# A hybrid decoder step on one core: the last chunk of the down pass takes four pairs, its products are staggered, and the residual stream lies in two tiles

## Chip, cores and metric

The kernel runs on one core of a Trainium2 chip. The metric is device time of one execution in microseconds; lower is better.

## The reference

One layer of a decoder on 1,024 prompt tokens and 64 sample tokens (1,088 rows of width 1,024), in float32:

```python
x = layer_norm(ALPHA * x + 0.5 * swiglu(x, f1_wg, f1_wu, f1_wd), ln1_g, ln1_b)
z = x @ w_in + b_in                 # split into u, v, q, k, vm, o, ig, fg
...                                 # gMLP groups and mLSTM heads on z -> mix
x = layer_norm(ALPHA * x + mix @ w_out, ln2_g, ln2_b)
x = layer_norm(ALPHA * x + 0.5 * swiglu(x, f2_wg, f2_wu, f2_wd), ln3_g, ln3_b)
```

with `swiglu(x, wg, wu, wd) = (silu(x @ wg) * (x @ wu)) @ wd` and a hidden width of 2,816.

## The kernel before

The rows are nine tiles of 128 tokens: 0 to 7 are the prompt, 8 holds the 64 sample tokens. Each feed-forward layer has an up pass (class `Up`, lines 340 to 400) and a down pass (class `Down` and function `down`). The hidden width is 22 blocks of 128, taken as 11 pairs.

Both passes use seven products of half matrices instead of eight (a Strassen-like scheme), numbered 1 to 7 and taken in the order `DOWN_ORDER = (1, 2, 6, 5, 3, 7, 4)`. A product has a left operand made of hidden activations (`hop`, written to memory by the up pass as `hw` and loaded back, 512 KB each) and a right operand made of weights (`wop`). Each operand is split into a high and a low part, so one product over one pair is three matmuls of 128x512 (`PROD`, line 682). The `wop` is made by a cast on ScalarE (line 221) and a subtraction on VectorE (line 222).

The 11 pairs are cut into chunks. Within a chunk, a round is one product number for four row blocks `i`: block `i` stands for tiles `i` and `i + 4`. The pairs of the chunk add up in PSUM, and at the end of each product VectorE adds the PSUM tile to the residual stream `y` (line 653). Products 1, 6, 7 and 4 of a block share one PSUM tile (`px`, named `pd`); 2, 5 and 3 take one of a ring of four (`pw`), and the sample tokens' products another of that ring (`psm`, line 691). Product 5 is added twice, to tile `i + 4` and to tile `i`; product 3 goes to tile `i`.

In the last chunk each tile's last addition also collects its sum (`finish`) and starts a background task that normalises the tile (`layer_norm`, lines 266 to 290): a sum of squares on ScalarE, a power on GpSimd, two whole-row operations on VectorE. After the first pass the task then transposes the tile on TensorE (line 235) and splits it into `xt`; after the second it stores the tile, and tile 7 alone goes by statistics in two halves (line 674). The sample tile is folded first (`fold_tail`, line 766). The projection that follows the first pass (`zunit`, line 872, PSUM `po`) takes the tiles one after the other and waits for each one's task.

Operands are prepared ahead: three `wop` (`DOWN_AHEAD`) beyond the round, from nine buffers, and `hop` by SyncE's queue two further on into a ring of eight. `y` is loaded from the residual in quarter-megabyte pieces at the beginning of a pass, into memory that the up pass has left. The Python code makes the instructions in the order of its loops, and a scheduler in the tile framework then orders each engine's queue; so what stands where is read from the built program.

Of the kernel before, what the change touches and what calls it, by code (L numbers as in the profile page):

```python
# [43 lines left out]
UP_ORDER = (1, 2, 6, 5, 7, 3, 4)  # L44
DOWN_ORDER = (1, 2, 6, 5, 3, 7, 4)
NPRE = 2
CHUNKS = ((0, 1), (2, 3, 4), (5, 6, 7), (8, 9, 10))
PROD = ((0, 0), (0, 1), (1, 0))
UP_AHEAD = 3
DOWN_AHEAD = 3  # L50
# [51 lines left out]
class Weights:  # L102
# [32 lines left out]
    def done(self, n):  # L135
        for i in range(self.finished, self.finished + n):
            self.tiles.pop(self.plan[i])
        self.finished += n
        self.fill()


class Background:
# [25 lines left out]
def trunk_kernel(ctx: ExitStack, tc: tile.TileContext, a):  # L168
# [39 lines left out]
    def psum_s(name):  # L208
        return pss.tile([P, 512], F32, tag="s", name=name)
# [335 lines left out]
    class Down:  # L545


        def __init__(self, ffn):
            self.ffn = ffn
            self.items = [(ci, m, pair) for ci, pairs in enumerate(CHUNKS) for m in DOWN_ORDER for pair in pairs]  # L550
            self.n = 0
            self.raws, self.t1s, self.ops, self.hsl, self.hops = {}, {}, {}, {}, {}
            self.ud = None

        def load(self, group):
            if group in self.raws or 2 * group >= NPAIR:
# [27 lines left out]

        def fetch(self, upto):
            while self.fetched < min(upto, len(self.items)):
                _, m, pair = self.items[self.fetched]
                self.hop_load(unit(self.ud, "hop", f"hop{pair}_{m}"), pair, m)
                self.fetched += 1

        def prepare(self, upto):
# [47 lines left out]
    def down(dn, residual, on_tile):  # L639
# [18 lines left out]
        for ci, pairs in enumerate(CHUNKS):  # L658
# [34 lines left out]
                                  skip_group_check=True)  # L693

            px = {}
            smp = None

            rounds = [[(m, i) for i in range(4)] for m in DOWN_ORDER]
            if last:
                rounds[5:] = [[(m, i) for i in range(4) for m in DOWN_ORDER[5:]]]  # L700
            for r, round_ in enumerate(rounds):
                ms = sorted({m for m, i in round_}, key=DOWN_ORDER.index)
                done[0] += len(pairs) * len(ms)
# [6 lines left out]
                if ci == 0 and r == 3:  # L710
                    load_y(residual, range(4, 8), (0,))
                late = ci == 0 and r < 2
                for sm in (() if late and r == 0 else (1, 2) if late else ms):
                    if sm in (1, 2, 3, 7):
                        if sm in (1, 3):
                            smp = psum_s("psm")
                        sample(smp, sm, {1: 0, 2: 1, 3: 2, 7: 0}[sm], sm in (1, 3))
                        if sm in (2, 7):
                            add(smp, 8, int(sm == 7))
                if last and 7 in ms:  # L720
                    sums8 = lnst.tile([P, 1], F32, tag="sums8", name="sums8", bufs=1)
                    bg.spawn("fold", fold_tail(sums8))
# [3 lines left out]
                for m, i in round_:  # L726
                    if m in (1, 6, 7, 4):
                        if m == 1:
                            px[i] = psum_z("pd")
                        p = px[i]  # L730
                        product(p, m, i, m == 1)
                    else:
                        p = psum_s("pw")
                        product(p, m, i, True)
                    if m == 1:
                        add(p, i, 0)
                    elif m == 2:
                        finish(p, i, 0)
                    elif m == 6:
                        add(p, i, 1)  # L740
                    elif m == 5:
                        add(p, i + 4, 1)
                        add(p, i, 1)
                    elif m == 3:
                        finish(p, i, 1)
                        if last:
                            bg.spawn(("ln", ffn + 1, i), on_tile(i, sums[i]))
                    elif m == 7:
                        finish(p, i + 4, 1)
                    else:  # L750
                        finish(p, i + 4, 0)
                        if last:
                            bg.spawn(("ln", ffn + 1, i + 4), on_tile(i + 4, sums[i + 4]))
                    bg.tick()
                for m in ms:
                    for pair in pairs:
                        dn.hops.pop((pair, m))
# [10 lines left out]

    def y_pool(name):
        yp = tc.alloc_tile_pool(name=name, bufs=1, reuse_waits="tile")  # L770
        st["y"] = yp.tile([P, NT, YW], F32, tag="y", name="y")
        return yp


# [157 lines left out]

    wts = token_weights("o", 0)
    G.memset(y[TS:P, 8, :], 0.0)
    for t in range(NT):
        rows = _rows(t)
        bg.until(("ln", 1, t))

        def evict(p, t=t, rows=rows):
            add_psum(t, zg[:rows, t, :], p[:, 0:8], gb[:rows])  # L940
            og = m2.tile([P, 256], F32, tag="og", name="og")
            add_psum(t, og[:rows], p[:, 8:264], bc1[:rows, 0:256])
            S.activation(y[:rows, t, 520:776], og[:rows], AF.Tanh, scale=0.5)

        zunit(t, wts, 264, evict, "po", release=t == 8)

    def gtile(name, shape=(NT, H)):
        return mx.tile([P] + list(shape), F32, tag="g_" + name, name="g_" + name)
# [292 lines left out]
    def epilogue_a(h):  # L1241
# [4 lines left out]
        V.reciprocal(dn, dn)  # L1246
        yield
        hv = hh[:, :, 0:P]
        yo = y[:, :, 520 + h * P:520 + (h + 1) * P]
        dnb = dn.unsqueeze(2).to_broadcast([P, NT, P])  # L1250
        if h == 2:
            V.tensor_tensor(yo, hv, dnb, op=ALU.mult)
        else:
            V.tensor_tensor(hv, hv, dnb, op=ALU.mult)
            yield
            if h == 3:
                while ("o", 1) not in bg.finished:
                    yield
            V.scalar_tensor_tensor(yo, yo, 1.0, hv, op0=ALU.add, op1=ALU.mult)
        yield  # L1260
        bg.spawn(("epb", h), epilogue_b(h))

# [397 lines left out]
```

## Time and profile before

| | us |
|---|---|
| median of three runs | 2012.18 (2011.77 to 2012.43) |
| profiled execution | 2008.55 |
| its span | 2006.8 |
| TensorE busy | 1945.1 (97%) |
| VectorE busy | 1333.6 (66%) |

The span is that of one execution under the hardware profiler, with times from its start; the first down pass runs from 482 to 739 us, the second from 1747 to 1993. A row of the timeline gives start, duration, engine, line and operation, what is written and read, the count of merged instructions, and in brackets the idle time just before them and what ended it. Matmuls overlap, so one reads longer (about 0.4 us) than the distance between two.

### The profile page before, as it was taken

The page shows a single profiled execution, that of the slowest core. Times are in us where ns is not written, and L with a number is a line of the kernel's source. Part 1 is how long each engine was busy: PE and PEld are TensorE (multiplying, and loading weights), DVE is VectorE, ACT ScalarE, POOL GpSimd, SP SyncE. Part 2 cuts the span into 40 slices and gives each one's busy share as a digit, 9 for nine tenths or more (in the row PEclk, how much of TensorE's full clock was granted, in tenths as well). Part 3 has the DMA queues.
Part 4 walks back from the last instruction along what each step waited for, and adds up shares of the span by engine and source line. Part 5 has one row for each costly group of instructions (what it writes and reads, how often), then busy time and mean ns, then how long its engine had stood idle before and what let it go on. Part 6 is the DMA issues. An engine that isn't in the chain of part 4 may idle for free.

```text
span 2006.8 us, 27421 instructions
## 1 busy us (share of the span) xinstructions
PE 1945.1 (97%) x10263; PEld 1648.5 (82%) x10263; DVE 1333.6 (66%) x2337; ACT 766.1 (38%) x1499; POOL 489.4 (24%) x404
## 2 busy tenths in 40 slices
PE   8999999998999989999999999999999999989996
PEld 7888888887788869888978999888888888868885
DVE  8866565665866594366775767986655565676558
ACT  6544444443222241154454233644444444322122
POOL 0222322223421130104332510113222222153112
PEclk9999999999999999999999999999999999999999
DMA  5444433348865552111111073234444433897554
GB/s 211 150 170 149 148 130 120 129 146 312 342 243 188 184 177 65 43 43 51 43 50 55 26 236 117 90 130 151 142 153 161 133 127 109 292 378 253 178 176 147
DMA packets 105501, 308.64 MB, mean 154 GB/s; under 512 B 19736, under 2 KB 27416, under 8 KB 102552
## 3 DMA queue, kind: packets, MB, share of 16 engines
q1 hardware_dynamic: 83192, 226.13, 34.2%
q10 hardware_dynamic: 22176, 80.75, 10.1%
q8 instruction: 81, 1.33, 0.3%
q14 instruction: 52, 0.43, 0.1%
HBM read 205.50 MB, written 101.34 MB: 153 GB/s over the span
## 4 chain that ended last, share of the span: by engine, by line
PE 82%; DVE 8%; DMA 3%; ACT 2%; POOL 2%; issue 2%; ACTq 0%; DVEq 0%; SPq 0%; POOLq 0%
PE px L364 23%; PE pw L364 12%; PE pd L682 11%; PE pw L682 8%; PE pz L364 6%; PE pw L872 4%; PE psm L380 4%; PE pq L892 4%; DMA hd<-hw 3%; PE pv L872 2%; PE po L872 2%; PE psm L691 2%; PE pgm L872 1%; DVE y L290 1%; PE tp L235 1%
## 5 line engine op out<-in xcount | busy, mean ns | idle before, releaser
L364 PE MATMUL px<-xo,uop 128*128 128x512 f32 x2112 | 504.5, 394 | 6.1 <-ACT uop L355 6.1
L364 PEld LDWEIGHTS px<-xo,uop 128*128 128x128 f32 x2112 | 392.4, 188 | 91.6 <-ACT uop L355 6.3
L682 PE MATMUL pd<-wop,hop 128*128 128x512 f32 x1056 | 255.4, 398 | 6.8 <-ACT wop L221 3.4
L356 DVE TENSOR_TENSOR uop<-ur,uop 128x512 fp32r<-128x512 f32 x264 | 187.2, 730 | 101.2 <-ACT uop L355 101.0
L364 PE MATMUL pw<-xo,uop 128*128 128x512 f32 x1056 | 250.0, 392 | 0.0
L682 PEld LDWEIGHTS pd<-wop,hop 128*128 128x128 f32 x1056 | 199.7, 190 | 55.1 <-ACT wop L221 4.3
L364 PEld LDWEIGHTS pw<-xo,uop 128*128 128x128 f32 x1056 | 198.1, 188 | 44.3
L682 PE MATMUL pw<-wop,hop 128*128 128x512 f32 x792 | 191.2, 397 | 8.8 <-DVE y L653 7.5
L355 ACT CAST uop<-ur 128x512 fp32r<-128x512 f32 x264 | 157.0, 620 | 97.4 <-PE psm L380 65.3
L682 PEld LDWEIGHTS pw<-wop,hop 128*128 128x128 f32 x792 | 149.5, 189 | 45.2 <-DVE y L653 8.4
L221 ACT CAST wop<-wd 128x512 fp32r<-128x512 f32 x132 | 80.9, 620 | 261.4 <-DVE y L653 187.1
L345 POOL TENSOR_TENSOR s<-ur,ur 128x1024 f32<-128x1024 f32 x18 | 43.3, 2403 | 509.6 <-DVE uop L356 436.3
L222 DVE TENSOR_TENSOR hw<-c,hw 128x512 fp32r<-128x512 f32 x132 | 108.0, 818 | 80.0 <-ACT hw L221 79.9
L653 DVE SCALAR_TENSOR_TENSOR y<-y,pd 128x512 f32<-128x512 f32 x128 | 85.9, 682 | 65.2 <-PE pd L682 65.1
L364 PE MATMUL pz<-xo,uop 128*128 128x512 f32 x528 | 127.7, 397 | 0.0
L222 DVE TENSOR_TENSOR wop<-wd,wop 128x512 fp32r<-128x512 f32 x132 | 108.5, 829 | 23.9 <-ACT wop L221 23.1
L221 ACT CAST hw<-c 128x512 fp32r<-128x512 f32 x132 | 82.0, 621 | 109.6 <-DVE c L470 48.1
L653 DVE SCALAR_TENSOR_TENSOR y<-y,pw 128x512 f32<-128x512 f32 x128 | 84.0, 684 | 55.6 <-PE pw L682 55.6
L364 PEld LDWEIGHTS pz<-xo,uop 128*128 128x128 f32 x528 | 97.5, 188 | 22.4
L380 PEld LDWEIGHTS psm<-uop,xs 128*128 128x128 f32 x704 | 95.3, 189 | 7.8 <-ACT uop L355 0.3
L872 PE MATMUL pgm<-w,xt 128*128 128x256 f32 x768 | 99.8, 287 | 1.8 <-POOL w L123 0.8
L872 PE MATMUL pw<-w,xt 128*128 128x256 f32 x768 | 99.2, 287 | 0.3 <-ACT xt L221 0.3
(299 smaller groups left out, 2878.6 us busy)
## 6 DMA issues: line engine op xcount, KB each, us to landing
hd<-hw ACTq DMA_DIRECT2D x154, 512.0 KB, 3.4
hop<-hd SPq DMA_DIRECT2D x154, 512.0 KB, 5.0
ur<-in_wu SPq DMA_DIRECT2D x94, 512.0 KB, 3.8
wd<-in_wd SPq DMA_DIRECT2D x22, 1024.0 KB, 8.5
wr<-in_ws SPq DMA_DIRECT2D x76, 256.0 KB, 2.9
hsd<-sm SPq DMA_DIRECT2D x22, 192.0 KB, 4.1
y<-in_x SPq DMA_DIRECT2D x16, 256.0 KB, 6.2
x1d<-y SPq DMA_DIRECT2D x8, 512.0 KB, 4.0
```

The lines of the kernel that those rows point to most:

```text
L221: S.copy(hi, src)
L222: V.tensor_sub(dst[ix + (1,)], src, hi.bitcast(F32))
L345: eng.tensor_tensor(s1, a21, a22, op=ALU.add)
L355: S.copy(op[:, 0], sj)
L356: V.tensor_sub(op[:, 1], sj, op[:, 0].bitcast(F32))
L364: TE.matmul(ps, lhsT=units[k // 2][:, wi, c0:c0 + P], rhs=self.xo[m][:, k, xi, :], start=start and k == 0 and j == 0, stop=k == 3 and j == ...
L380: TE.matmul(ps, lhsT=self.xs[:, which, k, :], rhs=units[k // 2][:, wi, (k % 2) * 256:(k % 2 + 1) * 256], start=first and k == 0 and wi == ...
L653: V.scalar_tensor_tensor(yv, yv, al, p, op0=ALU.mult, op1=ALU.add, **(dict(accum_out=accum) if accum is not None else {}))
L682: TE.matmul(p, lhsT=hop[:, hi, i * P:(i + 1) * P], rhs=wop[:, wi, :], start=start and pi == 0 and j == 0, stop=pi == len(pairs) - 1 and j ...
L691: TE.matmul(p, lhsT=hsl[pair][:, which, :], rhs=wop[:, wi, :], start=start and pi == 0 and wi == 0, stop=pi == len(pairs) - 1 and wi == 1, ...
L872: TE.matmul(p[:, :n], lhsT=xl(t, k, xi), rhs=wk[:, wi, kk * n:(kk + 1) * n], start=(i == 0), stop=(i == last - 1))
L892: TE.matmul(p[:, :n], lhsT=wk[:, wi, kk * P:(kk + 1) * P], rhs=rhs, start=(i == 0), stop=(i == (23 if c < 2 else 15)), skip_group_check=c ...
```

## The change

The chunks are cut at other places: 2, 3, 2 and 4 pairs instead of 2, 3, 3 and 3. In all chunks but the last, products 5 and 3 are one double round, staggered (5 of block 0, 5 of 1, 3 of 0, 5 of 2, 3 of 1, ...): product 3 accumulates in PSUM on top of product 5 after 5 has been added to tile `i + 4`, and tile `i` gets both in one addition. The sample products of that round move behind it. In the last chunk 7 and 4 are staggered in the same way, where the code took them alternately, and the `hop` of product 7 lie in one larger tile (`hopx`). `y` becomes two tiles, one for tiles 0 to 3 and one for 4 to 8, behind a small class that picks by tile; operations over all nine tiles are issued once for each part. The first projection takes tile 8 fifth instead of last.

```diff
-CHUNKS = ((0, 1), (2, 3, 4), (5, 6, 7), (8, 9, 10))
+CHUNKS = ((0, 1), (2, 3, 4), (5, 6), (7, 8, 9, 10))
...
+class Tokens:
+    def __getitem__(self, ix):
+        rows, t, cols = ix
+        return self.first[rows, t, cols] if t < 4 else self.second[rows, t - 4, cols]
+    def parts(self, cols):
+        return (slice(0, 4), self.first[:, :, cols]), (slice(4, NT), self.second[:, :, cols])
...
-                _, m, pair = self.items[self.fetched]
-                self.hop_load(unit(self.ud, "hop", f"hop{pair}_{m}"), pair, m)
+                ci, m, pair = self.items[self.fetched]
+                if ci == len(CHUNKS) - 1 and m == 7:
+                    if self.hopx is None:
+                        self.hopx = xa_tile(xap, "hopx")
+                    hop = self.hopx[:, pair - CHUNKS[-1][0]]
+                else:
+                    hop = unit(self.ud, "hop", f"hop{pair}_{m}")
+                self.hop_load(hop, pair, m)
...
+            def staggered(m1, m2):
+                return [(m1, 0)] + [x for i in range(3) for x in ((m1, i + 1), (m2, i))] + [(m2, 3)]
...
             if last:
-                rounds[5:] = [[(m, i) for i in range(4) for m in DOWN_ORDER[5:]]]
+                rounds[5:] = [staggered(*DOWN_ORDER[5:])]
+            else:
+                rounds[3:5] = [staggered(*DOWN_ORDER[3:5])]
+            pw = {}
...
+                if ms != [5, 3]:
+                    samples(() if late and r == 0 else (1, 2) if late else ms)
...
+                    elif m == 3 and not last:
+                        p = pw.pop(i)
+                        product(p, m, i, False)
                     else:
-                        p = psum_s("pw")
+                        p = pw[i] = psum_s("pw")
                         product(p, m, i, True)
...
                     elif m == 5:
                         add(p, i + 4, 1)
-                        add(p, i, 1)
+                        if last:
+                            add(p, i, 1)
...
+                if ms == [5, 3]:
+                    samples(ms)
...
-        st["y"] = yp.tile([P, NT, YW], F32, tag="y", name="y")
+        st["y"] = Tokens(yp.tile([P, 4, YW], F32, tag="ya", name="ya"), yp.tile([P, NT - 4, YW], F32, tag="yb", name="yb"))
...
-    for t in range(NT):
+    for t in (0, 1, 2, 3, 8, 4, 5, 6, 7):
...
-        zunit(t, wts, 264, evict, "po", release=t == 8)
+        zunit(t, wts, 264, evict, "po", release=t == 7)
...
-        yo = y[:, :, 520 + h * P:520 + (h + 1) * P]
+        yos = y.parts(slice(520 + h * P, 520 + (h + 1) * P))
...
-            V.scalar_tensor_tensor(yo, yo, 1.0, hv, op0=ALU.add, op1=ALU.mult)
+            for ts, yo in yos:
+                V.scalar_tensor_tensor(yo, yo, 1.0, hv[:, ts], op0=ALU.add, op1=ALU.mult)
```

Where instructions now stand is shown at three places. Lines of the changed kernel are 15 to 40 higher than before, and numbers behind a name tell buffers apart.

TensorE at the end of the first down pass, before: the last product of 4 (`pd_5274`, tile 7), then transposes (`tp`) of tiles 4, 5 and 6, then the projection (`po`) of tile 0 from `xt00` and `xt01`.

```order
L682 MATMUL pd_5274<-wop8_4_5617,hop8_4_5488 128x512 x3
L682 MATMUL pd_5274<-wop9_4_5621,hop9_4_5494 128x512 x3
L682 MATMUL pd_5274<-wop10_4_5625,hop10_4_5614 128x512 x3
L235 MATMUL tp_5744<-cc_76,y_3948 128x128 x4
L235 MATMUL tp_5755<-cc_76,y_3948 128x128 x4
L235 MATMUL tp_5789<-cc_76,y_3948 128x128 x4
L235 MATMUL tp_5799<-cc_76,y_3948 128x128 x4
L872 MATMUL po_6003<-w0_5875,xt00_5554 128x264
L235 MATMUL tp_5833<-cc_76,y_3948 128x128 x4
L235 MATMUL tp_5843<-cc_76,y_3948 128x128 x4
L872 MATMUL po_5904<-w0_5875,xt00_5554 128x264 x5
L872 MATMUL po_5904<-w1_5880,xt00_5554 128x264 x6
```

The same place in the changed kernel: `po_5863`, `po_5910` and `po_5941` are tiles 0, 1 and 2, and the transposes that read `yb` are those of tiles 4 and 5.

```order
L703 MATMUL pd_5135<-wop10_4_5573,hop10_4_5562 128x512 x3
L910 MATMUL po_5863<-w0_5834,xt00_5478 128x264 x4
L250 MATMUL tp_5714<-cc_76,yb_3949 128x128 x4
L250 MATMUL tp_5725<-cc_76,yb_3949 128x128 x4
L910 MATMUL po_5863<-w0_5834,xt00_5478 128x264 x2
L250 MATMUL tp_5765<-cc_76,yb_3949 128x128 x4
L250 MATMUL tp_5775<-cc_76,yb_3949 128x128 x4
L910 MATMUL po_5863<-w1_5839,xt00_5478 128x264 x6
L910 MATMUL po_5863<-w2_5844,xt01_5492 128x264 x6
L910 MATMUL po_5863<-w3_5849,xt01_5492 128x264 x6
L910 MATMUL po_5910<-w0_5834,xt00_5478 128x264 x6
L910 MATMUL po_5910<-w1_5839,xt00_5478 128x264 x6
```

The transposes of tiles 4 and 5 now stand between projection matmuls, and those of tile 6 have moved behind 59 of them, where before one stood ahead.

TensorE near the end of the second down pass, before: `pd_16935` is the PSUM tile of block 0, `pd_16946` of block 1, `pd_16957` of block 2 and `pd_16968` of block 3; the number behind `wop` and its pair is the product.

```order
L682 MATMUL pd_16957<-wop8_7_17179,hop8_7_17118 128x512 x3
L682 MATMUL pd_16957<-wop9_7_17185,hop9_7_17123 128x512 x3
L682 MATMUL pd_16957<-wop10_7_17191,hop10_7_17176 128x512 x3
L682 MATMUL pd_16968<-wop8_7_17179,hop8_7_17118 128x512 x3
L682 MATMUL pd_16968<-wop9_7_17185,hop9_7_17123 128x512 x3
L682 MATMUL pd_16968<-wop10_7_17191,hop10_7_17176 128x512 x3
L682 MATMUL pd_16935<-wop8_4_17281,hop8_4_17182 128x512 x3
L682 MATMUL pd_16935<-wop9_4_17285,hop9_4_17188 128x512 x3
L682 MATMUL pd_16935<-wop10_4_17289,hop10_4_17278 128x512 x3
L682 MATMUL pd_16946<-wop8_4_17281,hop8_4_17182 128x512 x3
L682 MATMUL pd_16946<-wop9_4_17285,hop9_4_17188 128x512 x3
L682 MATMUL pd_16946<-wop10_4_17289,hop10_4_17278 128x512 x3
```

In the changed kernel the four blocks' tiles are `pd_16765`, `pd_16779`, `pd_16793` and `pd_16807`, and each product is over four pairs.

```order
L703 MATMUL pd_16807<-wop7_7_17080,hopx_17009 128x512 x3
L703 MATMUL pd_16807<-wop8_7_17085,hopx_17009 128x512 x3
L703 MATMUL pd_16765<-wop7_4_17202,hop7_4_17088 128x512 x3
L703 MATMUL pd_16765<-wop8_4_17208,hop8_4_17193 128x512 x3
L703 MATMUL pd_16765<-wop9_4_17212,hop9_4_17199 128x512 x3
L703 MATMUL pd_16765<-wop10_4_17216,hop10_4_17205 128x512 x3
L703 MATMUL pd_16779<-wop7_4_17202,hop7_4_17088 128x512 x3
L703 MATMUL pd_16779<-wop8_4_17208,hop8_4_17193 128x512 x3
L703 MATMUL pd_16779<-wop9_4_17212,hop9_4_17199 128x512 x3
L703 MATMUL pd_16779<-wop10_4_17216,hop10_4_17205 128x512 x3
L703 MATMUL pd_16807<-wop9_7_17091,hopx_17009 128x512 x3
L703 MATMUL pd_16807<-wop10_7_17196,hopx_17009 128x512 x3
```

Product 4 of blocks 0 and 1 has moved ahead of the second half of product 7 of block 3; after product 4 of block 0 there are now 42 matmuls to the end, 27 before.

VectorE at the very end of the second pass, before: line 290 is the last step of a tile's normalisation, 287 the step before, 653 the addition of a product, and 674 to 283 the statistics and halves of tile 7.

```order
L290 SCALAR_TENSOR_TENSOR y_15643<-y_15643,bmv_17370,bc_ln3_b_17214 128x1024
L674 BN_STATS bst_17416<-y_15643 128x6
L226 TENSOR_SCALAR rsq_17406<-bmv_17400 128x1
L287 SCALAR_TENSOR_TENSOR y_15643<-y_15643,bmv_17400,bc_ln3_g_17212 128x1024
L653 SCALAR_TENSOR_TENSOR y_15643<-y_15643,pd_16968 128x512
L290 SCALAR_TENSOR_TENSOR y_15643<-y_15643,bmv_17400,bc_ln3_b_17214 128x1024
L674 BN_STATS bst_17416<-y_15643 128x6
L259 BN_AGGR bmv_17432<-bst_17416 128x2
L261 TENSOR_SCALAR bmv_17432<-bmv_17432 128x1
L226 TENSOR_SCALAR rsq_17436<-bmv_17432 128x1
L280 SCALAR_TENSOR_TENSOR y_15643<-y_15643,bmv_17432,bc_ln3_g_17212 128x512 x2
L283 SCALAR_TENSOR_TENSOR y_15643<-y_15643,bmv_17432,bc_ln3_b_17214 128x512 x2
```

In the changed kernel the same steps are lines 305, 302, 674 and 695 to 298; the first row is tile 7's last addition.

```order
L674 SCALAR_TENSOR_TENSOR yb_15622<-yb_15622,pd_16807 128x512
L283 SCALAR_TENSOR_TENSOR bmv_17361<-sums_17308,negd_79 128x1
L695 BN_STATS bst_17344<-yb_15622 128x6
L274 BN_AGGR bmv_17384<-bst_17344 128x2
L276 TENSOR_SCALAR bmv_17384<-bmv_17384 128x1
L295 SCALAR_TENSOR_TENSOR yb_15622<-yb_15622,bmv_17384,bc_ln3_g_17117 128x512
L241 TENSOR_SCALAR rsq_17367<-bmv_17361 128x1
L302 SCALAR_TENSOR_TENSOR yb_15622<-yb_15622,bmv_17361,bc_ln3_g_17117 128x1024
L241 TENSOR_SCALAR rsq_17388<-bmv_17384 128x1
L295 SCALAR_TENSOR_TENSOR yb_15622<-yb_15622,bmv_17384,bc_ln3_g_17117 128x512
L305 SCALAR_TENSOR_TENSOR yb_15622<-yb_15622,bmv_17361,bc_ln3_b_17119 128x1024
L298 SCALAR_TENSOR_TENSOR yb_15622<-yb_15622,bmv_17384,bc_ln3_b_17119 128x512 x2
```

Behind tile 7's last addition there now stand tile 6's normalisation (`bmv_17361`) and tile 7's own steps; before, the end of tile 5's (`bmv_17370`, the first row) and the first step of tile 6's (`bmv_17400`) stood ahead of that addition.

More of the change, by code (lines that the diff above doesn't have):

```diff
@@ L139, in done, with __init__ @@
         self.fill()
+class Tokens:
+    def __init__(self, first, second):
+        self.first, self.second = first, second
+    def __getitem__(self, ix):
[3 more added lines that the diff above has]
+        return (slice(0, 4), self.first[:, :, cols]), (slice(4, NT), self.second[:, :, cols])
 class Background:
@@ L552, in __init__ @@
             self.raws, self.t1s, self.ops, self.hsl, self.hops = {}, {}, {}, {}, {}
-            self.ud = None
+            self.ud = self.hopx = None
         def load(self, group):
@@ L695, in down @@
             px = {}
-            smp = None
+            smp = []
+            def staggered(m1, m2):
+                return [(m1, 0)] + [x for i in range(3) for x in ((m1, i + 1), (m2, i))] + [(m2, 3)]
             rounds = [[(m, i) for i in range(4)] for m in DOWN_ORDER]
             if last:
-                rounds[5:] = [[(m, i) for i in range(4) for m in DOWN_ORDER[5:]]]
+                rounds[5:] = [staggered(*DOWN_ORDER[5:])]
+            else:
+                rounds[3:5] = [staggered(*DOWN_ORDER[3:5])]
+            pw = {}
             for r, round_ in enumerate(rounds):
@@ L712, in down, with samples @@
                 late = ci == 0 and r < 2
[L713 to L719, printed above, removed]
+                def samples(sms):
+                    for sm in sms:
+                        if sm in (1, 2, 3, 7):
+                            if sm in (1, 3):
+                                smp.append(psum_s("psm"))
+                            sample(smp[-1], sm, {1: 0, 2: 1, 3: 2, 7: 0}[sm], sm in (1, 3))
+                            if sm in (2, 7):
+                                add(smp[-1], 8, int(sm == 7))
+                if ms != [5, 3]:
+                    samples(() if late and r == 0 else (1, 2) if late else ms)
                 if last and 7 in ms:
@@ L1248, in epilogue_a @@
         hv = hh[:, :, 0:P]
-        yo = y[:, :, 520 + h * P:520 + (h + 1) * P]
+        yos = y.parts(slice(520 + h * P, 520 + (h + 1) * P))
         dnb = dn.unsqueeze(2).to_broadcast([P, NT, P])
         if h == 2:
-            V.tensor_tensor(yo, hv, dnb, op=ALU.mult)
+            for ts, yo in yos:
+                V.tensor_tensor(yo, hv[:, ts], dnb[:, ts], op=ALU.mult)
         else:
@@ L1258, in epilogue_a @@
                     yield
-            V.scalar_tensor_tensor(yo, yo, 1.0, hv, op0=ALU.add, op1=ALU.mult)
+            for ts, yo in yos:
+                V.scalar_tensor_tensor(yo, yo, 1.0, hv[:, ts], op0=ALU.add, op1=ALU.mult)
         yield
```

## The prediction

> **What bounds the kernel now.** I read the page's head first, then the stretches of both down passes as windows, then TensorE in order of time wherever a window shows it idle, and last VectorE at those places. The head says that TensorE is the bound.
>
> ```profile
> span 2006.8 us, 27421 instructions
> PE 1945.1 (97%) x10263; PEld 1648.5 (82%) x10263; DVE 1333.6 (66%) x2337; ACT 766.1 (38%) x1499; POOL 489.4 (24%) x404
> ```
>
> Nothing in the change removes a matrix product, so it can only pay out of the 61.7 us in which TensorE is idle, or where the clock is low. The windows give stretch, length, busy time of TensorE (PE), weight loads, VectorE, ScalarE, GpSimd, and then the granted clock.
>
> ```profile
> 546.00:704.00 158.00, 158.00 (x682) 127.88 (x681) 95.36 (x144) 33.56 (x54) 33.60 (x22) 1.00 0.60 208
> 1810.00:1972.00 162.00, 162.00 (x703) 131.56 (x702) 98.02 (x150) 34.16 (x55) 33.69 (x23) 1.00 0.58 199
> 735.30:750.40 15.10, 7.29 (x39) 5.55 (x37) 14.91 (x26) 8.75 (x15) 6.84 (x21) 0.91 0.64 213
> 747.80:754.60 6.80, 5.83 (x27) 5.86 (x28) 6.39 (x9) 2.10 (x4) 0.76 (x5) 0.50 0.96 321
> 1982.30:1984.30 2.00, 0.02 (x2) 0.05 (x1) 2.00 (x7) 0.60 (x1) 0.00 (x0) 1.00 0.00 0
> 1992.90:2006.80 13.90, 0.00 (x0) 0.00 (x0) 10.36 (x18) 1.24 (x2) 3.87 (x3) 0.65 0.38 151
> ```
>
> The inner chunks of both passes have no gap at all (158 of 158, 162 of 162). The losses are where the first pass hands over to the projection (735 to 750: VectorE busy 14.91 of 15.10, TensorE 7.29), the 2 us at 1982, and the 13.9 us after the last matmul. VectorE ends the waits in all three; behind the first the clock is at half for 6.8 us.
>
> **The change part by part.**
>
> *Third product accumulated on the fifth, staggered.* Twelve additions per pass go (four in each of three chunks), 24 in all at 0.684 us, 16.4 us of VectorE.
>
> ```profile
> L653 DVE SCALAR_TENSOR_TENSOR y<-y,pw 128x512 f32<-128x512 f32 x128 | 84.0, 684 | 55.6 <-PE pw L682 55.6
> ```
>
> All lie in the inner chunks where TensorE never waits, and VectorE itself waits 55.6 us before this group: gain 0. What it may cost: the third product of a row of tokens now needs the fifth's first addition to have read the buffer. One other product stands between, six to nine matmuls at 0.231 us (16.64/72, the row next below), 1.4 to 2.1 us, against 0.68. The double round also keeps six operands (hop) in the ring of eight in the one three-pair chunk of each pass.
>
> ```profile
> 1910.17 16.64 PE pd L682 x72
> L567 SPq DMA_DIRECT2D hop<-hd x51: 319/320/873, 546.2 to 694.2; - x51
> DMA to landing us min/median/max: 3.5/4.4/6.3
> ```
>
> The third hop of product 3 can be loaded when the last product of round 6 frees a unit: 2.1 us, then two fifth products (4.2) and two thirds of the next (1.4), 7.7 us ahead of its use. Landing takes 4.4, at most 6.3. I take 0, bounds 0 and 3 us of loss (two such rounds).
>
> *Last chunk of four pairs.* The number of matmuls is the same. Three operands are prepared ahead of a round, so the fourth pair's cast and subtraction fall into the round.
>
> ```profile
> L221 ACT CAST wop<-wd 128x512 fp32r<-128x512 f32 x132 | 80.9, 620 | 261.4 <-DVE y L653 187.1 <-PE pd L682 43.4 <-PE pw L682 16.5
> L222 DVE TENSOR_TENSOR wop<-wd,wop 128x512 fp32r<-128x512 f32 x132 | 108.5, 829 | 23.9 <-ACT wop L221 23.1
> ```
>
> That is 1.45 us; the first product reaches its fourth pair after 9 matmuls, 2.1 us, and with seven of nine operand buffers in use the two engines may begin before the round does. I take 0; bounds 0 and 0.6 us at each of ten round heads, 6 us.
>
> *Hand-over of the first pass.* Seven waits, of which these are the rows (the eighth is the slow run of projection matmuls behind them, the last the same at full clock).
>
> ```profile
> 722.45 1.09 PE L235 MATMUL tp<-cc,y 128*128 128x128 f32 x8 [0.67 <-DVE rsq L226]
> 727.32 1.06 PE L235 MATMUL tp<-cc,y 128*128 128x128 f32 x8 [1.47 <-DVE bmv L266]
> 736.38 0.36 PE L872 MATMUL po<-w,xt 128*128 128x264 f32 x1 [0.64 <-DVE y L653]
> 736.90 2.37 PE L682 MATMUL pd<-wop,hop 128*128 128x512 f32 x9 [0.16 <-DVE y L653]
> 740.70 2.26 PE L235 MATMUL tp<-cc,y 128*128 128x128 f32 x16 [1.43 <-DVE y L290]
> 744.84 0.36 PE L872 MATMUL po<-w,xt 128*128 128x264 f32 x1 [1.89 <-DVE rsq L226]
> 748.77 1.94 PE L235 MATMUL tp<-cc,y 128*128 128x128 f32 x8 [3.57 <-DVE y L290]
> 750.36 10.49 PE L872 MATMUL po<-w,xt 128*128 128x264 f32 x69
> 762.83 13.34 PE L872 MATMUL po<-w,xt 128*128 128x264 f32 x108
> 732.70 0.67 DVE L653 SCALAR_TENSOR_TENSOR y<-y,pd 128x512 f32<-128x512 f32 x1
> 735.54 0.69 DVE L653 SCALAR_TENSOR_TENSOR y<-y,pd 128x512 f32<-128x512 f32 x1 [0.19 <-PE pd L682]
> ```
>
> They sum to 9.83 us. Now the transposes of tiles 4 to 6 stand ahead of nearly all projection matmuls, so TensorE sits until VectorE has normalised those tiles. In the changed order they stand between projection matmuls of tiles 0 to 3 and 8. I place each against E, the end of the last down product.
>
> Tile 4: its addition at 732.70 to its transposes at 740.70 was 8.0 us. Its last product now ends 40 matmuls (9.2) and eight short transposes (0.7) before E, its transposes come 0.5 after: covered. Tile 5: its addition follows 0.6 later and its transposes 1.1 later, 8.5 us; its last product ends 28 matmuls, 6.5 us, before E, its transposes stand 1.6 after: wait 0.4. Tile 6: 735.54 to 748.77 was 13.2; now 2.8 before E (12 matmuls) and 59 projection matmuls (13.34/108 = 0.124 each, 7.3) and 16 transposes (2.1) after, 12.2: wait 1.0. So 1.4 us are left, a gain of 8.4. If tiles 4 and 5 also took 13.2, the three would wait up to 5 us together: bounds 4.8 and 9.8.
>
> The clock: 69 matmuls took 10.49 where 69 x 0.124 = 8.5, and eight transposes 1.94 where the row at 722 has 1.09. With no wait over 1.0 us I expect no low clock: gain 2.8, bounds 0 and 3.5. The Trainium skill (TensorE: Matmul & The Clock Gate, section on the HAM clock gate) says that the clock is halved after an idle window of about 3.4 us, windows running free of the program. By it the 6.8 us at half would give back 3.4 instead of 2.8; the trace agrees in that half clock begins at the 3.57 us wait.
>
> *Round of 7 and 4 in the second pass.*
>
> ```profile
> 1984.29 8.56 PE L682 MATMUL pd<-wop,hop 128*128 128x512 f32 x36 [1.98 <-issue]
> 1983.51 0.67 DVE L653 SCALAR_TENSOR_TENSOR y<-y,pd 128x512 f32<-128x512 f32 x1
> ```
>
> The first product of 4 waited for the addition of 7 at 1983.51, which stood behind normalisations of tiles 0 to 3. Now 50 matmuls instead of 42 stand between (1.85 us more), and round 3 gives VectorE 2.77 instead of 2.08 us a tile (2.8 us less backlog); against it three subtractions come in ahead (2.5). 1.98 - 1.85 - 2.8 + 2.5 is below 0; I leave 0.3: gain 1.7, bounds 0 and 2.
>
> *After the last matmul* (1984.29 + 8.56 = 1992.85) VectorE works until the last row here ends at 2003.64, 10.8 us, and the store takes 3.2.
>
> ```profile
> 1993.19 1.27 DVE L287 SCALAR_TENSOR_TENSOR y<-y,bmv,bc_ln_g 128x1024 f32<-128x1024 f32 x1
> 1996.11 0.69 DVE L674 BATCH_NORM_STATS2 bst<-y 128x6 f32<-128x512 f32 x1
> 1997.96 0.68 DVE L653 SCALAR_TENSOR_TENSOR y<-y,pd 128x512 f32<-128x512 f32 x1
> 2000.47 0.21 DVE L259 BATCH_NORM_AGGREGATE bmv<-bst 128x2 f32<-128x12 f32 x1
> 2002.23 1.41 DVE L283 SCALAR_TENSOR_TENSOR y<-y,bmv,bc_ln_b 128x512 f32<-128x512 f32 x2
> ```
>
> Tile 5's normalisation and all of tile 6's lie in it. In the new order the product of tile 4 ends 42 matmuls (9.7 us) before E instead of 27 (6.2), that of tile 5 30 instead of 18, so both are done by E. What is left: addition of tile 7 (0.6), its statistics (0.7) and aggregation (0.4), four half rows at about 0.7 (2.8), two whole rows of tile 6 (2.4), five tiny steps and their latencies (0.9): 7.8. Gain 3.0, bounds 1.5 and 3.5.
>
> *Two tiles for the residual stream.* The first pass also has waits at its start:
>
> ```profile
> 499.64 2.92 PE L682 MATMUL pw<-wop,hop 128*128 128x512 f32 x6 [5.40 <-DVE y L653]
> SPq L637 <- PE pw L364: 8.9, 1, 8.9
> ```
>
> The residual's loads wait for product 3 of the up pass, whose operand lies where y goes. The first half, 4 x 1040 x 4 = 16,640 bytes a partition, is 256 bytes longer than an operand tile and still touches the next, so its first load still waits: gain 0, and 5.4 us if it did not. The split VectorE operations of the heads (one more for each of four heads) run beside a busy TensorE: 0.
>
> Sum: 8.4 + 2.8 + 1.7 + 3.0 = 15.9 us. The profiled execution took 2008.55 us, of which the span is 2006.8; it becomes 1990.9 in span and 1992.65 in all. The median of the runs is 3.63 above that execution, so 2012.18 - 15.9 = 1996.3.
>
> **The rivals.** *The hand-over stays VectorE-bound* (chance 0.14): VectorE was busy 14.91 of 15.10 us there and no normalisation is removed. For it: the same work per tile. Against it: the five tiles' projection is 13.8 us of ready matmuls. With waits of 5 and the low clock kept: 4.8 + 0 + 1.7 + 3.0 = 9.5 us, 2002.7.
>
> *The fourth pair's operand comes late* (0.05), the case on the other side: ten round heads. It decides once cast and subtraction end more than 2.1 us after the head; each us beyond costs 10 us, so at 2.1 us beyond (the subtraction behind three queued additions) 21 us are lost and 2017 results. Against it: VectorE is busy 95.36 of 158.
>
> *The residual does load early* (0.04): another 5.4 us in the first pass, about 1991.
>
> *It does not do what it says* (0.05): the waits at the three places move elsewhere and come to the same, 2012. Against it: three separate places would have to.
>
> *The clock falls all the same.* By the skill's rule the windows run free of the program; scattered transposes could still make one window count as idle. In this kernel that is 2.8 us back, 1999.1, a chance of 0.1 within the forecast's range.
>
> **How the numbers follow.** The forecast as argued, 1993 to 2000, has 0.72. The range is 1991 to 2004: below it takes in the upper bounds (9.8 + 3.5 + 2 + 3.5 = 18.8, 1993.4) and most of an early residual; above it the VectorE-bound hand-over. A measurement tells 0.2%, some 4 us, from no change. Faster by more is the forecast, the early residual and the VectorE-bound hand-over: 0.91. Same: 0.05. Slower: 0.04.
>
> **What would show it.** Right: between the end of the first down pass and the projection TensorE waits under 2 us and the granted clock stays at 1.00; no row of about 2 us ahead of product 4 in the second pass; about 11 us from the last matmul to the end of the span. Additions at the residual number 24 fewer, with the windows of the inner chunks still full. Wrong: waits of product 3 on hop or on an operand's cast, or waits of the spread transposes over 3 us.

## The result, and the profile after

The median fell from 2011.99 to 1997.2 us, by 14.8 us; the two medians alone give a ratio of 0.9926. The ratio over all runs of the two kernels, with its 95% interval, is 0.9916 (0.9894 to 0.9937), and a second comparison gave 0.9908 (0.9894 to 0.9923), with a median of 1992.63 us. The forecast was 1996.3. Two executions far outside the rest, 4901 us of the kernel before and 2726 us of the one with the old chunks, are left out of the ratios here and below. The profiled execution took 1990.98 us, its span 1989.2, where the one before had 2008.55 and 2006.8. Head of the page after:

```profile
span 1989.2 us, 27420 instructions
PE 1939.1 (97%) x10263; PEld 1643.8 (83%) x10263; DVE 1318.4 (66%) x2317; ACT 764.0 (38%) x1499; POOL 482.9 (24%) x404
```

VectorE is 15 us less busy; the 24 additions less stand for 16.4, and a few split operations came in. Two windows inside the passes, the hand-over and the time after the last matmul, with the same columns as in the prediction:

```profile
546.00:704.00 158.00, 158.00 (x687) 127.74 (x686) 94.60 (x146) 33.64 (x55) 34.46 (x24) 1.00 0.62 220
1795.00:1955.00 160.00, 160.00 (x693) 129.62 (x692) 98.08 (x150) 35.32 (x58) 34.77 (x25) 1.00 0.60 210
729.00:744.00 15.00, 13.95 (x101) 12.85 (x100) 14.41 (x24) 8.58 (x17) 8.69 (x19) 1.00 0.67 218
1977.90:1989.20 11.30, 0.00 (x0) 0.00 (x0) 7.45 (x15) 1.24 (x2) 2.18 (x2) 0.68 0.35 139
```

The inner chunks are as full as before. In the 15 us of the hand-over VectorE is as busy as it was (14.41, was 14.91), but TensorE now works 13.95 us of them instead of 7.29, at full clock; both windows begin about 4 us ahead of the end of the last product. TensorE there in order of time:

```profile
732.72 0.65 PE L910 MATMUL po<-w,xt 128*128 128x264 f32 x4
733.21 1.04 PE L250 MATMUL tp<-cc,yb 128*128 128x128 f32 x8
734.01 0.49 PE L910 MATMUL po<-w,xt 128*128 128x264 f32 x2
735.44 1.07 PE L250 MATMUL tp<-cc,yb 128*128 128x128 f32 x8 [0.94 <-DVE yb L305]
736.26 6.66 PE L910 MATMUL po<-w,xt 128*128 128x264 f32 x53
743.04 1.06 PE L250 MATMUL tp<-cc,yb 128*128 128x128 f32 x8
```

One wait of 0.94 us (tile 5) is left of 9.83 us. At the end of the second pass the last product 4 waits 0.21 us, where the first had waited 1.98:

```profile
1974.81 3.06 PE L703 MATMUL pd<-wop,hop 128*128 128x512 f32 x12 [0.21 <-DVE rsq L241]
```

VectorE's last row of the program:

```profile
1984.05 1.41 DVE L298 SCALAR_TENSOR_TENSOR yb<-yb,bmv,bc_ln_b 128x512 f32<-128x512 f32 x2
```

Where the 17.6 us of span went is read from windows over whole stages: the first pass with the projection of `o`, the middle up to the second pass, and the second pass to its last matmul. Before, then after:

```profile
482.50:777.97 295.47, 278.13 (x1298) 227.79 (x1296) 198.94 (x321) 78.67 (x135) 83.58 (x99) 0.97 0.63 222
777.97:1747.16 969.19, 953.01 (x5726) 837.05 (x5725) 639.17 (x1281) 405.40 (x874) 229.98 (x209) 0.99 0.33 109
1747.16:1992.85 245.69, 237.57 (x1017) 190.63 (x1015) 169.59 (x265) 59.21 (x97) 70.79 (x47) 0.99 0.66 236
```

```profile
482.40:762.90 280.50, 272.67 (x1297) 224.16 (x1296) 188.97 (x311) 78.30 (x136) 80.87 (x100) 0.99 0.65 234
762.90:1729.68 966.78, 950.49 (x5725) 835.37 (x5724) 636.58 (x1282) 404.66 (x873) 227.26 (x209) 0.99 0.33 110
1729.68:1977.87 248.19, 239.52 (x1017) 191.48 (x1015) 167.48 (x256) 58.50 (x97) 71.46 (x48) 0.99 0.65 235
```

Length less PE's busy time is its idle time. The first pass lost 15.0 us: 9.5 of idle (17.3 to 7.8) and 5.5 by which the same matmuls were busy for less time, the clock being 0.99 instead of 0.97. The middle, where no instruction for TensorE changed, got 2.4 us shorter at the same idle time. The second pass got 2.5 us longer (0.55 of idle, 1.95 in slower matmuls), and the time after it 2.6 shorter. So in these two executions the gain lies in the first pass and the end; the 1.8 us won ahead of product 4 went back at the start of the second pass, where waits of 2.15, 1.98, 0.99 and 1.01 us had stood and these stand now, 8.36 together:

```profile
1745.97 2.47 PE L703 MATMUL pw<-wop,hop 128*128 128x512 f32 x6 [4.54 <-DVE yb L674]
1758.06 0.50 PE L703 MATMUL pd<-wop,hop 128*128 128x512 f32 x1 [2.83 <-ACT wop L236]
1759.55 4.37 PE L703 MATMUL pd<-wop,hop 128*128 128x512 f32 x11 [0.99 <-DVE wop L237]
```

### The profile page after: what moved, and what is told of

Its sections match the earlier page's. It is cut to its first block, busy times and chain, and to the rows that moved or that the text cites. A ratio compares the mean times of both kernels' runs of the same rounds, so it can differ in the third digit from the quotient of the medians.

```text
span 1989.2 us, 27420 instructions
## 1 busy us (share of the span) xinstructions
PE 1939.1 (97%) x10263; PEld 1643.8 (83%) x10263; DVE 1318.4 (66%) x2317; ACT 764.0 (38%) x1499; POOL 482.9 (24%) x404
## 4 chain that ended last, share of the span: by engine, by line
PE 52%; DVE 5%; DMA 2%; POOL 2%; issue 1%; ACT 1%; ACTq 0%; DVEq 0%; POOLq 0%
PE px L379 11%; PE pw L379 6%; PE pd L703 5%; PE pgm L910 4%; PE pq L930 4%; PE pw L703 4%; PE pw L910 4%; PE pz L379 3%; PE pv L910 2%; PE psm L395 2%; PE po L910 2%; DMA hd<-hw 2%; PE psm L712 1%; PE tp L250 1%; DVE yb L305 1%
## 5 line engine op out<-in xcount | busy, mean ns | idle before, releaser
L703 PE MATMUL pd<-wop,hop 128*128 128x512 f32 x960 | 233.6, 400 | 8.4 <-ACT wop L236 6.1
L703 PEld LDWEIGHTS pd<-wop,hop 128*128 128x128 f32 x960 | 182.5, 191 | 53.2 <-ACT wop L236 7.0
L395 PE MATMUL psm<-uop,xs 128*128 128x256 f32 x704 | 97.9, 281 | 0.0
L930 PE MATMUL pq<-xt,w 128*128 128x512 f32 x384 | 96.7, 403 | 0.0
```

Source lines behind the costliest of these rows:

```text
L395: TE.matmul(ps, lhsT=self.xs[:, which, k, :], rhs=units[k // 2][:, wi, (k % 2) * 256:(k % 2 + 1) * 256], start=first and k == 0 and wi == ...
L703: TE.matmul(p, lhsT=hop[:, hi, i * P:(i + 1) * P], rhs=wop[:, wi, :], start=start and pi == 0 and j == 0, stop=pi == len(pairs) - 1 and j ...
L930: TE.matmul(p[:, :n], lhsT=wk[:, wi, kk * P:(kk + 1) * P], rhs=rhs, start=(i == 0), stop=(i == (23 if c < 2 else 15)), skip_group_check=c ...
```

## The experiments

Ratios are to the kernel before, run beside each. The waits are TensorE's in the profiled execution of each kernel, in us, those at the hand-over from 700 to 765 us.

| kernel | ratio (95%) | waits at the hand-over | wait before product 4 | after last matmul |
|---|---|---|---|---|
| before | 1 | 9.83 | 1.98 | 13.9 |
| changed | 0.9916 (0.9894 to 0.9937) | 0.94 | 0.21 | 11.3 |
| without accumulating 3 on 5 | 0.9919 (0.9905 to 0.9932) | 0.94 | 0.21 | 11.4 |
| with one tile for `y` | 0.9893 (0.9880 to 0.9907) | 0.95 | 0.21 | 11.4 |
| with tile 8 last | 0.9919 (0.9906 to 0.9932) | 0.94 | 0.21 | 11.3 |
| with the old chunks | 0.9999 (0.9985 to 1.0013) | 8.96 | 1.91 | 14.0 |
| before + new chunks | 0.9968 (0.9957 to 0.9979) | 2.77 | 7.58 | 7.8 |
| with 7 and 4 alternated | 0.9935 (0.9922 to 0.9949) | 2.55 | 3.78 | 7.8 |
| before + new chunks + stagger | 0.9946 (0.9933 to 0.9959) | 2.74 | 0 | 15.4 |
| without `hopx` | 0.9935 (0.9922 to 0.9948) | 2.56 | 0 | 15.4 |
| three store buffers | 0.9894 (0.9881 to 0.9908) | 0.94 | 0.21 | 11.3 |
| stores through `raw` | 0.9855 (0.9842 to 0.9869) | 0.95 | 0.21 | 11.3 |

**The parts that do nothing.** Three kernels undo one part each. Products 5 and 3 apart again:

```diff
-            else:
-                rounds[3:5] = [staggered(*DOWN_ORDER[3:5])]
...
-                    elif m == 3 and not last:
-                        p = pw.pop(i)
-                        product(p, m, i, False)
...
-                        if last:
-                            add(p, i, 1)
+                        add(p, i, 1)
```

> The changed kernel with products 5 and 3 as two rounds and two PSUM tiles again, the 24 additions (16.4 us of VectorE) back. My theory (the gain is at the hand-over and the end, from the chunk of four pairs with the staggered 7 and 4): no change, 1997 (ratio 0.992), inner chunks without gaps. Rival 'VectorE relief' (the saved additions are what pays): slower than the changed kernel by a good part of 16.4 us, 2005 to 2013, with new waits in the inner chunks.

One tile for the residual stream, with all else as it was:

```diff
-        st["y"] = Tokens(yp.tile([P, 4, YW], F32, tag="ya", name="ya"), yp.tile([P, NT - 4, YW], F32, tag="yb", name="yb"))
+        whole = yp.tile([P, NT, YW], F32, tag="y", name="y")
+        st["y"] = Tokens(whole[:, 0:4], whole[:, 4:NT])
```

> The changed kernel with the residual stream in one tile, the same slices and the same split operations. My theory: no change, 1997 (ratio 0.992), since the first half already touches the last operand tile of the up pass by 256 bytes. Rival 'finer dependencies' (two tiles let loads and additions of the one half go on beside the other): slower by the 2 to 5 us that the first product 2 of each down pass then waits more (2.50 and 4.54 us with two tiles).

And tile 8 last in the projection:

```diff
-    for t in (0, 1, 2, 3, 8, 4, 5, 6, 7):
+    for t in range(NT):
...
-        zunit(t, wts, 264, evict, "po", release=t == 7)
+        zunit(t, wts, 264, evict, "po", release=t == 8)
```

> The changed kernel with tile 8 last in the first projection. Its 16 matmuls of 264 columns (about 2 us) then stand behind tiles 4 to 7 and no longer ahead of them. Where the projection of tiles 4 to 7 is late with its operands, 1 to 2 us are lost; my theory: tile 6 had a wait under 1 us and is the only one near its limit, so no change that can be measured, ratio 0.991 to 0.992. Rival (the place of tile 8 is part of the cure): 2 us more, ratio 0.993.

All three keep the gain. The window of the inner chunks without the accumulation, and then its groups of additions:

```profile
546.00:704.00 158.00, 158.00 (x688) 127.96 (x686) 98.97 (x153) 33.57 (x54) 33.61 (x23) 1.00 0.62 218
```

```profile
L674 DVE SCALAR_TENSOR_TENSOR ya<-ya,pw 128x512 f32<-128x512 f32 x96 | 65.3, 683 | 39.9 <-PE pw L703 39.9
L674 DVE SCALAR_TENSOR_TENSOR yb<-yb,pw 128x512 f32<-128x512 f32 x32 | 21.9, 685 | 12.3 <-PE pw L703 12.1
```

There are 128 additions from `pw` again; VectorE works 4.4 us more in this window, and TensorE still all of it. So 16.4 us of VectorE work bought nothing that these runs can tell. With one tile the ratio is even a little lower (0.9893), by about the width of an interval. With tile 8 last the wait at the hand-over is 0.94 us too.

**The cut.** The changed kernel with the chunks of before:

```diff
-CHUNKS = ((0, 1), (2, 3, 4), (5, 6), (7, 8, 9, 10))
+CHUNKS = ((0, 1), (2, 3, 4), (5, 6, 7), (8, 9, 10))
```

> The changed kernel with chunks of 2, 3, 3 and 3 pairs again; stagger, accumulation, two tiles and the place of tile 8 stay. My theory: the hand-over of the first pass is back (waits of 8 to 10 us together where the changed kernel has 1.2, and the half clock behind it), the wait of 2 us ahead of product 4 in the second pass too, and 13 to 14 us after the last matmul where there are 11.3: 2008 to 2012, ratio 0.998 to 1.000. Rivals 'VectorE relief' and 'finer dependencies': the gain stays, 1997 to 2002.

The gain is gone. TensorE at its hand-over, and then a window over it:

```profile
741.53 3.14 PE L250 MATMUL tp<-cc,yb 128*128 128x128 f32 x16 [2.14 <-DVE yb L305]
745.67 0.56 PE L910 MATMUL po<-w,xt 128*128 128x264 f32 x1 [1.00 <-DVE rsq L241]
749.60 0.66 PE L250 MATMUL tp<-cc,yb 128*128 128x128 f32 x2 [3.37 <-DVE yb L305]
```

```profile
735.00:752.00 17.00, 10.21 (x45) 8.04 (x45) 16.71 (x30) 8.70 (x16) 7.71 (x26) 0.71 0.55 160
```

The waits of before are back to within about 1 us, and the low clock behind them (0.71 over 17 us). Nothing else in the change moves the time without the cut. The stagger does not even reach TensorE there: with the old chunks the scheduler puts all 36 matmuls of product 7 ahead of all 36 of product 4, as in the kernel before.

**The cut alone.** The kernel before, with the new `CHUNKS` line only:

> The kernel before with chunks of 2, 3, 2 and 4 pairs and nothing else; products 7 and 4 of the last chunk stay alternated. Theory C (the cut alone does it): the whole gain, ratio 0.991. My theory now (the cut and the stagger are needed together): the hand-over of the first pass is cured by the cut alone, about 12 us, since the products of tiles 4 to 6 end earlier and the spread transposes come from the scheduler. But with 7 and 4 of a block next to each other, product 4 waits for the addition of 7, which stands behind the normalisation of tiles 0 to 3 on VectorE: a wait of 4 to 8 us there in the second pass (1.98 before, 0.21 in the changed kernel). The time after the last matmul shrinks to some 8 us, because VectorE caught up during that wait. Together 2000 to 2004, ratio 0.995.

And the changed kernel with 7 and 4 alternated again:

```diff
-                rounds[5:] = [staggered(*DOWN_ORDER[5:])]
+                rounds[5:] = [[(m, i) for i in range(4) for m in DOWN_ORDER[5:]]]
```

> The changed kernel with 7 and 4 of the last chunk alternated as before and all else kept. My theory: the same wait as in the run with the cut alone, 4 to 6 us ahead of product 4 in the second pass, and 8 us instead of 11.3 after the last matmul; in the first pass up to 1.4 us more ahead of tile 6's transposes. About 3 us over the changed kernel, ratio 0.993 to 0.994. Rival (the cut is enough): ratio 0.991.

With the cut alone the waits at the hand-over fall from 9.83 to 2.77 us, and this is the longest of them:

```profile
736.39 0.68 PE L235 MATMUL tp<-cc,y 64*128 64x64 f32 x8 [1.31 <-DVE rsq L226]
```

TensorE near the end of the second pass, the cut alone first, then the alternated one:

```profile
1987.28 5.26 PE L682 MATMUL pd<-wop,hop 128*128 128x512 f32 x12 [7.58 <-DVE rsq L226]
```

```profile
1977.40 4.42 PE L703 MATMUL pd<-wop,hop 128*128 128x512 f32 x12 [3.78 <-DVE rsq L241]
```

The waits (4 to 8 us expected for the first, 4 to 6 for the second) and the shorter end came at about the expected size; the cut alone kept a little less than expected (2005.65 us, ratio 0.997 instead of 0.995), and the alternated kernel has the expected ratio (0.9935). Both runs join what I had as two terms: the wait before product 4 and the time after the last matmul are one backlog of VectorE. Their sum is 15.9 us before and with the old chunks, 15.3 to 15.4 with the cut alone or with cut and stagger, 11.5 in the changed kernel and 11.6 with 7 and 4 alternated. The stagger moves the backlog from the wait to the end, where no matmul stands behind it (the last 12 took 3.06 us in the changed kernel, 4.42 and 5.26 behind the waits, with a granted clock of 0.64 over the 4.42); it does not shorten it. What does is the next part.

**Cut and stagger alone.** The kernel before with these two:

> The kernel before with two parts of the change: chunks of 2, 3, 2 and 4 pairs and the staggered 7 and 4. No accumulation of 3 on 5, one tile for the residual stream, tile 8 last in the projection, product 7's hop in the ring. My theory: all of the gain, 1991 to 1999, ratio 0.991 to 0.993, no wait over 1 us at either hand-over. If the parts left out carry some of it, 2001 or more.

I expected all of the gain, and it kept some 60% of it (5.4 of 8 to 9 thousandths). Its 15.4 us after the last matmul led to the part that I had not priced, `hopx`. The changed kernel without it:

```diff
-                if ci == len(CHUNKS) - 1 and m == 7:
+                if False:
```

> The changed kernel with product 7's operands of the last chunk in the ring of eight instead of the larger tile hopx; all else as changed. In the run with the cut and the stagger alone the copy of the sample tile (sh, which takes a unit of that ring) came at 1973.05 us, 7.6 us ahead of the last matmul's end, where the changed kernel has it at 1959.78, 18 us ahead; VectorE then normalised the sample tile among tiles 4 to 7, 15.4 us remained after the last matmul instead of 11.3, and tile 6's transposes waited 2.56 instead of 0.94 us. Theory D (hopx frees the ring for sh): the same here, 15 us after the last matmul, 2 to 3 us at the hand-over, 4 to 6 us slower than the changed kernel, ratio 0.994 to 0.995. Rival (the accumulation, the two tiles or the place of tile 8 make that difference): 11.3 us after the last matmul and ratio 0.991 to 0.992.

```profile
737.73 0.68 PE L250 MATMUL tp<-cc,yb 64*128 64x64 f32 x8 [2.56 <-DVE yb L305]
1961.01 22.37 PE L703 MATMUL pd<-wop,hop 128*128 128x512 f32 x96
```

```profile
L802 ACT COPY sh<-yb x2: 1046/1046/1046, 726.7 to 1975.8; 64x1024 f32<-64x1024 f32 x2
  PE pd L703: 14.4, 2
```

The first two rows are TensorE at the hand-over and at the end, the other two the view of the tile `sh`: its two copies, and what ScalarE sat waiting for ahead of them. The sample tile's fold (`fold_tail`) takes a unit of the ring of eight. Products 7 and 4 over four pairs fill that ring, so the copy waits for matmuls to free a unit and comes 7.6 us ahead of the last matmul's end (1983.4). In the changed kernel, `hopx` leaves units free:

```profile
L802 ACT COPY sh<-yb x2: 1050/1050/1051, 712.8 to 1959.8; 64x1024 f32<-64x1024 f32 x2
```

That is 18.1 us ahead of the end (1977.9), and the sample tile's normalisation is done before those of tiles 4 to 7 crowd VectorE. `hopx` is worth 4.1 us after the last matmul and 1.6 at the hand-over, where without it the sample tile's transposes (64 rows) are what waits. Theory D held; the intervals of the two ratios overlap, so it is the traces that show it. The shortage is one that the four pairs bring: with three, in the kernel before, the copy at 1980.0 waits for no matmul, and with the old chunks `hopx` leaves the sum at 15.9.

**The spread.** The changed kernel's times lay between 1991 and 2000, wider than the first three of before (2011.77 to 2012.43). Sixteen later runs of the kernel before spread as far, from 2005 to 2015, so the spread is not the change's.

> The changed kernel once more, for a second profile and the spread of its times (1991.0 to 2000.4 in six runs, in two groups at 1991 and 1997 to 2000). Theory A: the spread is the clock. Each stretch of half clock of 3.41 us costs 1.7 us; a profile near 1998 would have about four such stretches more than the profiled 1991.0 (which has eight), with the waits themselves unchanged within 1 us. Theory B: the spread is waits on transfers at the start of the down passes (2.50, 3.28, 4.54 and 2.83 us in the first profile), which then are longer by 7 us together, at the same clock. Median expected 1997, ratio to the kernel before 0.992.

This profiled run took 1996.09 us (span 1994.3). Its middle stage:

```profile
763.44:1735.00 971.56, 955.97 (x5725) 840.27 (x5724) 637.53 (x1282) 405.13 (x873) 227.34 (x209) 0.98 0.33 109
```

4.8 of the 5.1 us more lie here, in a stage with the same instructions; the idle time is not longer (15.6, was 16.3), the matmuls are 5.5 us longer, at a clock of 0.98. The first pass differs by 0.8, the second by 0.2. That is theory A: the clock, in a stage that the change does not touch.

**What the change left.** Behind the waits at the start of both passes, the timeline of ScalarE of the changed kernel shows the casts of `hw`, on their way to memory through two buffers:

```profile
1743.38 0.62 ACT L236 CAST hw<-cs 128x512 fp32r<-128x512 f32 x1 [6.82 <-DMA hd<-hw]
1745.73 0.62 ACT L236 CAST hw<-c 128x512 fp32r<-128x512 f32 x1 [0.70 <-DMA hd<-hw]
1750.19 0.62 ACT L236 CAST hw<-c 128x512 fp32r<-128x512 f32 x1 [2.37 <-DMA hd<-hw]
1755.65 0.62 ACT L236 CAST hw<-c 128x512 fp32r<-128x512 f32 x1 [2.50 <-DMA hd<-hw]
```

Each waits until an earlier store has landed, and the casts of `wop` that TensorE needs stand behind it. VectorE's subtraction waits for the same cast, and the additions that free `pw` stand behind that. The kernel before had this chain too. There the wait of 5.40 us in the first pass ended at 499.64; ScalarE and VectorE ahead of it:

```profile
497.04 0.62 ACT L221 CAST hw<-cs 128x512 fp32r<-128x512 f32 x1 [7.47 <-DMA hd<-hw]
```

```profile
497.69 0.69 DVE L222 TENSOR_TENSOR hw<-cs,hw 128x512 fp32r<-128x512 f32 x1 [4.38 <-ACT hw L221]
498.90 0.68 DVE L653 SCALAR_TENSOR_TENSOR y<-y,psm 128x512 f32<-128x512 f32 x1
```

Three buffers instead of two:

```diff
-                hop = unit(self.stg, "stg", f"hw{pair}_{m}", 2)
+                hop = unit(self.stg, "stg", f"hw{pair}_{m}", 3)
```

> The changed kernel with three instead of two buffers (hw) for the hidden operands on their way to memory. What the change left are waits at the start of both down passes, 6.8 us in the first and 8.4 in the second, by the profile put down to an addition and to casts of wop. Theory E: behind them stands ScalarE, whose queue waits for the stores of the last pair's hw (6.82, 0.70, 2.37 and 2.50 us in the second pass, rows released by the store hd<-hw), and the casts of wop stand behind it. Then a third buffer takes one store's landing (3 to 6 us) out of each pass's chain: 3 to 6 us less in all, 1989 to 1994. Rival (the residual's loads are late): no change, 1992 to 1997.

And four of the last pair's seven operands put into the six buffers of `raw`, the ring of the up pass's weights:

```diff
-                hop = unit(self.stg, "stg", f"hw{pair}_{m}", 2)
+                if pair == NPAIR - 1 and n % 3:
+                    hop = unit(self.u2, "raw", f"hw{pair}_{m}", 6)
+                else:
+                    hop = unit(self.stg, "stg", f"hw{pair}_{m}", 2)
```

> The changed kernel in which four of the seven hidden operands of the last pair go through buffers of the weights' ring (raw), which holds nothing more by then; the other three keep the two buffers. Theory E: no cast of hw waits for a store any more; the waits of 15.1 us at the start of the two down passes shrink to what VectorE and the residual's loads need, some 5 to 7 us together, and with them one or two of the half-clock stretches of 3.41 us (1.7 us each): 8 to 13 us less than the changed kernel, 1981 to 1988, ratio 0.985 to 0.989. Rival (the residual's loads are late): the waits stay as they are, 1992 to 1997.

First the longest wait of a cast of `hw` in the second pass with three buffers, then the last cast with `raw`:

```profile
1739.39 0.62 ACT L236 CAST hw<-c 128x512 fp32r<-128x512 f32 x1 [5.50 <-DMA hd<-hw]
1734.59 0.61 ACT L236 CAST hw<-c 128x512 fp32r<-128x512 f32 x1
```

TensorE with `raw`, at the start of the first pass and then of the second:

```profile
497.93 1.95 PE L706 MATMUL pw<-wop,hop 128*128 128x512 f32 x6 [3.22 <-DVE yb L677]
1740.89 2.35 PE L706 MATMUL pw<-wop,hop 128*128 128x512 f32 x6 [1.87 <-DVE yb L677]
1752.37 10.24 PE L706 MATMUL pw<-wop,hop 128*128 128x512 f32 x43 [1.54 <-DMA hop<-hd]
```

With `raw` the last cast of `hw` comes at 1734.59 and waits for nothing (1755.65 in the changed kernel). The waits of the second pass fall from 8.36 to 3.41 us, those of the first from 6.77 to 4.42; there the first wait stays (3.22, was 2.50, and 3.95 in the second profile of the changed kernel) and the later ones shrink. The median is 1982.32 us (1980.69 to 1983.72), the lowest of all kernels, and by the ratios 11 to 12 us under the changed kernel (0.9855 to its 0.9908 and 0.9916). That is more than the 7.3 us of waits; the granted clock was 0.990 to 0.992 in its five runs and 0.984 to 0.991 in the changed kernel's eleven, which fits the rest but was not taken apart. Theory E held here: no cast of `hw` waits for a store, and 7.8 us of waits are left at the two starts, where 5 to 7 were expected. With three buffers it is not shown: the median of 1990.43 lies where the theory put it, but the casts still wait for stores, and the waits at the two starts are 13.8 us against 15.1. The two profiles of the changed kernel differ by more than that (15.1 and 16.8), and the kernel with one tile, with two buffers, has 13.6 and the same ratio. What holds up the additions behind the remaining 3.22 us was not tried. In the trace no load stands ahead of them, but two subtractions of `hw` that took 3.03 us together, where one takes 0.68 elsewhere.

## Why the prediction was right, point by point

*Hand-over, 8.4 expected:* 8.9 (9.83 to 0.94). The place was off by one: I had 1.0 us ahead of tile 6 and 0.4 ahead of tile 5, and it is tile 5 that waits, while tile 6 was ready behind its 53 matmuls.

*Clock behind it, 2.8 expected (0 to 3.5):* 2.9, an estimate from the window in the prediction, whose 5.83 us of busy time at a clock of 0.50 are now at 1.00. The rest of the 5.5 us by which the matmuls of the first pass took less time lies elsewhere, and no step of mine took it in. Some of it is at the start of the pass, where the granted clock from 482 to 546 us rose from 0.92 to 0.95; what remains was not traced.

*Product 4, 1.7 expected:* 1.77. *After the last matmul, 3.0 expected:* 2.6. Both sizes were right, but the step behind the second was not. I derived it from the order of VectorE's tail and from 42 matmuls in place of 27 after tile 4's product. With the same cut and stagger and no `hopx` that time is 15.4, not 11. The step that failed is "Last chunk of four pairs", where I priced the fourth pair's operands and not the ring that the sample tile's fold shares with them; the right number came from an order in which `hopx` had already done its work.

*Zeros:* accumulation, two tiles, split operations and the fourth pair's cast cost and bring nothing that these runs can tell, as argued. The window from 546 to 704 us is full in every variant, TensorE of the changed kernel waits nowhere in the last chunk of the second pass ahead of product 4, and the stage with the split operations has the same idle time as before (16.2 and 16.3 us); they were not tried alone.

*The sum* of 15.9 stands against 17.6 in the profiled pair and 0.84 to 0.92% of 2012 us (17 to 18.5) in the two comparisons. It left out what is not the change's: 2.4 us less in the middle and some 2 us more waiting at the start of the second pass, which nearly cancel. That the forecast met the median within 1 us is luck in part: the changed kernel's own median was 1997.2 in one comparison and 1992.6 in the other.

*The rivals:* VectorE stayed as busy at the hand-over as the first rival says, and it did not matter, since ready matmuls stood beside it. The clock did not fall at the hand-over. Waits that move elsewhere did come, within the second pass, with the cut alone. The chances for a faster kernel add up to 0.90, not 0.91, and those for a slower one to 0.05. The early residual did not come, and its price was read wrongly. I put the 5.40 us at the start of the pass down to the residual's loads, since an addition ended it; two rows further back in the same profile stand ScalarE's cast and the store that it waits for, and the run with `raw`, which leaves the loads as they are, cut the waits by half, though not the one of this place (3.22 us in that run).

## What to carry to other kernels

Waits that stand on one engine at two places, one ahead of a late product and one after the last, can be one backlog: add them up before giving an edit credit for either. An edit that takes a larger chunk also takes more of every ring; look for the rare user of that ring (here one copy per pass) before pricing the common ones. When a wait on the busiest engine names an addition or a cast, follow the queue of the engine that makes it one step further: here it ended at a store and two buffers. The Trainium skill (Trainium Kernel Development and Optimization, section Best Practices) says to double-buffer; this kernel had two buffers there. A third gave no gain that can be told from the spread, and the borrowed ones, by the ratios, 11 to 12 us.

## What was not expected of the hardware

The same wait does not always cost the same clock. The sample tile's transposes waited 2.56 us at the hand-over both in the run without `hopx` and in the run with cut and stagger alone. In the first, then the second, the window behind that wait:

```profile
737.00:744.00 7.00, 6.27 (x42) 6.24 (x43) 6.84 (x10) 1.82 (x4) 4.57 (x13) 0.76 0.90 301
```

```profile
736.90:744.00 7.10, 7.08 (x62) 7.03 (x63) 6.93 (x12) 2.30 (x6) 4.14 (x10) 1.00 1.00 317
```

One fell to 0.76 over 7 us and got 42 matmuls done, the other stayed at 1.00 and got 62. The first window begins 0.73 us ahead of the end of the wait; seven us from that end have 48 matmuls, at 0.76 too. The Trainium skill (TensorE: Matmul & The Clock Gate, Part 1 on the HAM clock gate) says that the window of about 3.4 us runs free of the program, which agrees with a price that depends on where the wait falls; it also speaks of a whole idle window, and here a wait of 2.56 us, shorter than that and with no other beside it, was enough. What the low clock added is 0 and about 1.7 us here (0.24 of 7 us) and 2.9 behind the wait of 3.57 us in the kernel before, estimates from the windows. A wait of a few microseconds is better priced as itself plus an uncertain 0 to 3 us than as a fixed sum.
